# Sixty-four bytes: moving a feed-forward pool and every second staged weight tile in SBUF

## The chip, the core and the metric

The kernel runs on one core of a Trainium2 chip. It is one program: one launch takes all inputs from HBM and leaves the layer's output in HBM. The metric is the device time of one execution in microseconds. Before the change three runs gave 2179.68, 2176.11 and 2177.18 us, a median of 2177.18 us.

The engines are named as in the profile: PE (TensorE, matmuls), PEld (TensorE's loads of the stationary operand), DVE (VectorE), ACT (ScalarE), POOL (GpSimd) and SP (SyncE, which issues most DMAs here).

## The reference

One decoder layer on 512 tokens of width 2048, in float32:

```
mod = silu(c) @ w_ada + b_ada                       # six vectors of 2048
h   = rms_norm(x) * (1 + scale1) + shift1
u   = h @ w_in                                      # conv group, q, six k/v groups, gates
y   = [rms_norm(conv(u)) | rms_norm(nsa_attention(u))]
x   = x + gate1 * (y @ w_out)                       # 2048 x 2048
h   = rms_norm(x) * (1 + scale2) + shift2
x   = x + gate2 * (relu(h @ w_ff1)^2 @ w_ff2)       # 2048 x 8192, 8192 x 2048
out = rms_norm(x)
```

Most of the arithmetic is in the last two products, the feed-forward.

## The kernel before

**Precision.** Every float32 matrix is split into a high part (rounded to the type float32r) and a low part (the rest). A product of two such matrices is three matmuls into the same PSUM bank: high by high, high by low, low by high (`mm3`, L345). ACT makes the high part by a copy, DVE the low part by a subtraction.

**Operands of a matmul.** `matmul(ps, lhsT, rhs)` loads `lhsT`, 128 columns, as the stationary operand and streams `rhs`, the moving operand, past it. The profile writes a matmul as out<-moving,stationary: `pf<-tk,hl` streams tokens past feed-forward weights. In nearly all matmuls the moving operand holds tokens and the stationary one weights. In one part of the projection, the value projection (rows `ps<-wh,h` and `ps<-wl,h_m` of shape 128x268), it is the other way round: the staged weights move, 268 columns at a time, and the tokens are stationary.

**Where tiles lie.** Pools lie one behind the other in each partition of SBUF, in the order in which they are opened, and the tiles' widths give their places:

- `mainp` (L279) has 29 slots of 4096 bytes, from byte 34,816 on. Token tiles of every stage live there: `h_m`, `mix`, `mixa`, and the feed-forward's tokens `tk` (L1142).
- `attc` and `stage` follow at byte 153,600. `stage` (L283) has two pairs of tiles `wh` and `wl` (L300) and three tiles `raw` (L301), each 1088 floats, 4352 bytes. The first pair lies at 169,472 and 178,176, the second at 173,824 and 182,528. Seven token tiles `h` lie behind them.
- When the front of the layer is done, `attc` and `stage` are closed, and `ffp` (L1040), the feed-forward's pool, opens at the same byte 153,600. It holds the arriving weights `rw` (six tiles), their split parts `hl` (three tiles of a high and a low half) and `sg`, `gt`, `gb` and `p1`. All its widths are multiples of 1024 bytes.

34,816 and 153,600 are both multiples of 1024, and token slots and the offsets used within them are multiples of 512 bytes. So in the feed-forward the moving and the stationary operand of every matmul start at the same place within any 128 bytes. In the front the same holds for tokens and staged weights, but for the value projection: there a weight tile is 1072 floats, four pieces of 268 columns, so that the four pieces start 0, 1072, 2144 and 3216 bytes into the tile. Within 64 bytes these are the offsets 0, 48, 32 and 16, within 128 bytes 0, 48, 96 and 16; the token tiles, stationary there, start at 0.

**Order of the work.** An object `Order` records every operation and writes the program in an order that a planner finds by costs and due times (`price`, `plan`, `emit`). Its costs depend on shapes and on which tile names an operation touches, not on addresses. The front comes first (modulation vectors from `w_ada`, projections, attention, first half of the output projection), then from about 770 us on the feed-forward's part, which starts with the second half of the output projection.

**The feed-forward.** The two products are done by a scheme of seven products of half-size blocks. For each of 32 blocks (`ff1`, L1244) four weight tiles arrive in `rw`, DVE and ACT make seven split operands in `hl` from them (`operands`, L1197), and TensorE runs 24 matmuls of 256 columns for each (`run`, L1213). Results pass through `gt` to HBM and come back as tokens `tk` for the second product, which is built the same way. In the three blocks done first and in the last block of the second product, some operands lie in `sg` and `gt`, or in slots (`kw`).

Of the kernel before, what the change touches and what calls it, by code (L numbers as in the profile page):

```python
# [9 lines left out]
F32 = mybir.dt.float32  # L10
F32R = mybir.dt.float32r
# [5 lines left out]
P = 128  # L17
# [11 lines left out]
BLOB = 1072  # L29
SLOT = 1024  # L30
WIDE = 1088
VEC_W = 336 + 88
CST_W = 1281 - 1024 + 80
NMAIN = 29
# [238 lines left out]
def hybrid_layer(ctx: ExitStack, tc: tile.TileContext, a, out):  # L273
# [9 lines left out]
    stage = front.enter_context(tc.tile_pool(name="stage", bufs=2))  # L283

    def slot(dtype=F32, name="m"):
        return mainp.tile([P, SLOT], dtype, name=name, tag="m")
# [10 lines left out]
    vcmp = attc.tile([P, NG, 2, P], F32R, name="vcmp")  # L297
    ident_r = attc.tile([P, P], F32R, name="ident_r")
    mask_r = attc.tile([P, P], F32R, name="mask_r")
    whl = cycle([[stage.tile([P, WIDE], F32R, name=n)[:, :BLOB] for n in ("wh", "wl")] for _ in range(2)])  # L300
    wraw = cycle([stage.tile([P, WIDE], F32, name="raw", bufs=3)[:, :BLOB] for _ in range(3)])  # L301
    accs = cycle([small.tile([P, 2], F32, name="acc") for _ in range(4)])

    def temp(shape=(P, T), dtype=F32, name=None):
        t = next(temps)[:, :math.prod(shape[1:])].bitcast(dtype)
        if len(shape) == 4:
            return t.rearrange("p (a b c) -> p a b c", b=shape[2], c=shape[3])
        return t if len(shape) == 2 else t.rearrange("p (a b) -> p a b", b=shape[2])
# [23 lines left out]
    def weights(src, cols=1024, spare=False):  # L332
        raw = next(wraw)[:, :cols]
        nc.sync.dma_start(out=raw, in_=src)
        wh, wl = (slot(F32R, name="sw") for _ in range(2)) if spare else next(whl)
        wh, wl = wh[:, :cols], wl[:, :cols]
        nc.scalar.activation(wh, raw, AF.Copy)
        nc.vector.tensor_tensor(out=wl, in0=raw, in1=wh.bitcast(F32), op=OP.subtract)
        return wh, wl
# [10 lines left out]

    vec = consts.tile([P, VEC_W], F32, name="vec")[:, :V_END]
    nc.sync.dma_start(out=vec, in_=a["vec"][:, :V_END])
# [234 lines left out]
    for s, (name, k) in enumerate(steps[:-1]):  # L587
# [5 lines left out]
        wh, wl = w  # L593
# [167 lines left out]
    for j in range(8):  # L761
# [4 lines left out]
        for i in range(3):  # L766
            n = 3 * j + i
# [30 lines left out]
    for g in range(NG):  # L798
        pv = [bank() for _ in range(NQ)]
        for blk in range(4):  # L800
            wh, wl = weights(a["w_v"][g * 4 + blk], BLOB)
# [47 lines left out]
    for g in range(NG):  # L849
        pq = [bank() for _ in range(NR)]  # L850
        for k in range(NK):
            if k % 2 == 0:
                wh, wl = weights(a["w_q"][g * 8 + k // 2])
# [175 lines left out]
    while m < NK:  # L1029
# [10 lines left out]
    ffp = ffn.enter_context(tc.tile_pool(name="ffp", bufs=2, reuse_waits="tile"))  # L1040
    psf = ffn.enter_context(tc.tile_pool(name="psf", bufs=8, space=PSUM, reuse_waits="tile"))
    HT = T // 2
    rw = cycle([ffp.tile([P, 1024], F32, name="rw", bufs=6) for _ in range(6)])
    hl = cycle([ffp.tile([P, 2, 1024], F32R, name="hl", bufs=3) for _ in range(3)])
    sg = {t: cycle([ffp.tile([P, 1024], d, name="sg", bufs=2) for _ in range(2)])
          for t, d in (("first", F32R), ("sums", F32), ("last", F32R))}
    gt = cycle([ffp.tile([P, 2, 2, HT], F32R, name="gt", bufs=3) for _ in range(3)])
    gb = cycle([ffp.tile([P, 2, HT], F32R, name="gb", bufs=1)])
    p1s = cycle([ffp.tile([P, HT], F32, name="p1", bufs=3) for _ in range(3)])
    banks = cycle([psf.tile([P, T], F32, name="pf") for _ in range(8)])  # L1050
    LO, HI = slice(0, HT), slice(HT, T)
    halves = (LO, HI)
# [5 lines left out]
    def raw_blob(src):  # L1058
        raw = next(rw)
        nc.sync.dma_start(out=raw, in_=src)  # L1060
        return raw

    def hl_tile():
        t = next(hl)
        return t[:, 0], t[:, 1]

    def hilo(dst, src, minus=False):
        if minus:
            nc.scalar.activation(dst[0], src, AF.Copy, scale=-1.0)
            nc.vector.scalar_tensor_tensor(out=dst[1], in0=src, scalar=-1.0, in1=dst[0].bitcast(F32),  # L1070
                                           op0=OP.mult, op1=OP.subtract)
        else:
            nc.scalar.activation(dst[0], src, AF.Copy)
            nc.vector.tensor_tensor(out=dst[1], in0=src, in1=dst[0].bitcast(F32), op=OP.subtract)
        return dst
# [20 lines left out]
    for k in range(8):  # L1096
        wh, wl = oa[k] if k < 2 else hilo(hl_tile(), raw_blob(a["w_oa"][k]))
# [44 lines left out]
    def tslot():  # L1142
        return slot(F32R, name="tk")[:, :4 * HT].rearrange("p (k h t) -> p k h t", k=2, h=2)

# [7 lines left out]
    def normed(kp, hf):  # L1152
        c = halves[hf]
        x = x1[kp]
        t = temp((P, 2, HT), name="xr")
        nc.vector.tensor_tensor(out=t, in0=x[:, :, c], in1=r2[:, None, c].to_broadcast([P, 2, HT]),
# [252 lines left out]
    for f in range(8):  # L1409
# [7 lines left out]
        for q in range(3 if last else 4):  # L1417
            raw = [raw_blob(a["w_f2"][4 * f + q, b]) for b in range(4)]
# [127 lines left out]
```

## Time and profile before

| What | Value |
|---|---|
| median of three runs | 2177.18 us |
| the profiled execution's own time | 2177.84 us |
| its span, first to last instruction | 2176.1 us |
| TensorE clock granted over the span | 0.993 |
| PE busy | 2121.7 us, 98% |
| PEld busy | 1979.9 us, 91% |
| DVE busy | 1899.1 us, 87% |
| ACT busy | 1006.3 us, 46% |
| matmuls | 15,014 |

The span and what lies around it, 1.7 us, make the profiled execution's time, which is 0.7 us above the median. Matmuls are pipelined: each has a duration longer than its distance from the next, so distances between starts are what counts, and "PE busy" is the union of overlapping intervals. In a row of a timeline or of a chain, the time divided by the count behind the x is that distance.

### The profile page before, as it was taken

How to read it: one execution, taken by the hardware profiler on the slowest of the kernel's cores; microseconds unless marked ns; L12 is line 12 of the kernel's file. 1: busy time of each engine (PE TensorE's matmuls, PEld its weight loads, DVE VectorE, ACT ScalarE, POOL GpSimd, SP SyncE). 2: the span in 40 equal slices, each digit the busy share in tenths (PEclk: the TensorE clock that was granted, in tenths of full speed). 3: DMA queues.
4: the chain of work that ended last, by engine and by line, in shares of the span. 5: the costliest groups of instructions: out<-in, count | busy, mean ns of one | idle time of the engine just before them, and what ended most of it. 6: DMA issues, size and time to landing. Idle time of an engine off the chain costs nothing.

```text
span 2176.1 us, 37941 instructions
## 1 busy us (share of the span) xinstructions
PE 2121.7 (98%) x15014; PEld 1979.9 (91%) x15014; DVE 1899.1 (87%) x2971; ACT 1006.3 (46%) x1470; POOL 128.2 (6%) x244
## 2 busy tenths in 40 slices
PE   5999999999999999999999999999999999999997
PEld 3888778898777789999999999999999999999997
DVE  8999888888977646998898898898999999999997
ACT  4532333222544435766566566555433333333344
POOL 0000000000000000111111111111000000000000
PEclk8999999999999999999999999999999999999998
DMA  8996688877220253566656656669866366366442
GB/s 334 336 352 225 216 298 335 304 285 284 80 78 30 68 205 115 173 202 193 207 191 190 213 186 192 205 186 314 302 246 234 121 236 232 126 224 234 135 174 88
DMA packets 144129, 454.16 MB, mean 209 GB/s; under 512 B 15824, under 2 KB 20176, under 8 KB 143952
## 3 DMA queue, kind: packets, MB, share of 16 engines
q1 hardware_dynamic: 108816, 386.72, 50.8%
q0 software_dynamic: 34048, 63.98, 9.3%
q8 instruction: 118, 1.93, 0.4%
q10 hardware_dynamic: 1088, 1.05, 0.1%
q14 instruction: 59, 0.48, 0.1%
HBM read 383.53 MB, written 68.16 MB: 208 GB/s over the span
## 4 chain that ended last, share of the span: by engine, by line
PE 81%; DVE 4%; DMA 2%; ACT 1%; issue 1%; SPq 0%; DVEq 0%; ACTq 0%
PE pf L119 64%; PE ps L119 11%; PE pw L119 3%; PE pv L119 1%; DMA wa<-in_w_ada 1%; PE s L119 1%; PE pt L119 1%; DVE nm L119 1%; DMA raw<-in_cmp_w 1%; DVE t L119 0%; DVE wl L119 0%; DVE p L119 0%; DVE tt L119 0%; DVE x L119 0%; DVE sw L119 0%
## 5 line engine op out<-in xcount | busy, mean ns | idle before, releaser
L119 PE MATMUL pf<-tk,hl 128*128 128x256 f32 x10704 | 1286.8, 283 | 0.5 <-ACT t L119 0.5
L119 PEld LDWEIGHTS pf<-tk,hl 128*128 128x128 f32 x10704 | 1285.4, 192 | 0.8 <-ACT t L119 0.7
L119 ACT ACTIVATE hl<-rw 128x1024 fp32r<-128x1024 f32 x269 | 284.7, 1059 | 366.4 <-PE pf L119 264.7
L119 DVE TENSOR_TENSOR hl<-rw,hl 128x1024 fp32r<-128x1024 f32 x269 | 328.8, 1223 | 51.9 <-ACT hl L119 51.4
L119 ACT ACTIVATE hl<-sg 128x1024 fp32r<-128x1024 f32 x180 | 190.9, 1060 | 260.6 <-PE pf L119 216.2
L119 DVE SCALAR_TENSOR_TENSOR t<-wa,cs 128x1024 bf16<-128x1024 f32 x192 | 234.5, 1221 | 32.5 <-DMA wa<-in_w_ada 30.1
L119 PE MATMUL ps<-h_m,wh 128*128 128x512 f32 x720 | 223.7, 391 | 0.0
L119 ACT ACTIVATE wh<-raw 128x1024 fp32r<-128x1024 f32 (+1 forms) x106 | 112.6, 1063 | 238.5 <-PE ps L119 189.2
L119 DVE TENSOR_TENSOR hl<-sg,hl 128x1024 fp32r<-128x1024 f32 x151 | 184.8, 1224 | 40.2 <-ACT hl L119 37.5
L119 PE MATMUL ps<-h,wh 128*128 128x512 f32 x560 | 176.8, 396 | 6.4 <-ACT h L119 3.3
L119 PEld LDWEIGHTS ps<-h_m,wh 128*128 128x128 f32 x720 | 134.8, 188 | 27.5
L119 DVE SCALAR_TENSOR_TENSOR x<-pf,mod,x 128x256 f32<-128x256 f32 (+1 forms) x280 | 135.3, 488 | 23.4 <-PE pf L119 20.4
L119 DVE TENSOR_TENSOR sg<-sg,rw 128x1024 f32<-128x1024 f32 x120 | 146.1, 1218 | 0.1
L119 DVE TENSOR_TENSOR wl<-raw,wh 128x1024 fp32r<-128x1024 f32 (+1 forms) x106 | 130.0, 1226 | 13.8 <-ACT wh L119 13.1
L119 PE MATMUL ps<-h_m,wl 128*128 128x512 f32 x360 | 141.0, 392 | 0.0
L119 PEld LDWEIGHTS ps<-h,wh 128*128 128x128 f32 x560 | 106.2, 191 | 31.9 <-ACT h L119 5.3
L119 POOL DMA_DIRECT2D g<-gt x192 | 101.2, 532 | 372.5 <-issue 149.4
L119 PE MATMUL ps<-h,wl 128*128 128x512 f32 x280 | 110.5, 395 | 0.0
L119 PE MATMUL pw<-mix,wh 128*128 128x512 f32 x256 | 86.4, 403 | 0.0
L119 PEld LDWEIGHTS ps<-h_m,wl 128*128 128x128 f32 x360 | 67.8, 188 | 14.2 <-DVE wl L119 0.3
L119 ACT ACTIVATE t<-t 128x512 f32<-128x512 f32 (+3 forms) x131 | 74.5, 571 | 11.5 <-DVE t L119 9.5
L119 DVE TENSOR_TENSOR sg<-rw 128x1024 f32<-128x1024 f32 x60 | 73.2, 1219 | 5.4 <-issue 2.7
(216 smaller groups left out, 2155.2 us busy)
## 6 DMA issues: line engine op xcount, KB each, us to landing
rw<-in_w_f SPq DMA_DIRECT2D x263, 512.0 KB, 3.7
wa<-in_w_ada SPq DMA_DIRECT2D x192, 512.0 KB, 6.4
tk<-g SPq DMA_DIRECT2D x114, 512.0 KB, 6.1
g<-gt POOLq DMA_DIRECT2D x192, 256.0 KB, 3.3
raw<-in_w_conv SPq DMA_DIRECT2D x32, 512.0 KB, 4.8
x<-in_xt SPq DMA_DIRECT2D x16, 512.0 KB, 5.5
raw<-in_w_kv SPq DMA_DIRECT2D x16, 512.0 KB, 5.3
raw<-in_w_cv SPq DMA_DIRECT2D x16, 512.0 KB, 3.8
```

The costliest lines, as they stand in the source:

```text
L119: x.i, x.eng, x.call = len(self.nodes), eng, (lambda: real(*args, **kw))
```

## The change

Two things are moved in SBUF; no operation is added or taken away.

- `ffp` gets a tile of 16 floats as its first one, which nothing uses. Everything else in `ffp` then lies 64 bytes further: `rw`, `hl`, `sg`, `gt`, `gb`, `p1`. The token slots stay.
- A pair `wh`, `wl` becomes one tile of 2 x 1088 + 16 floats, 8768 bytes; the low part starts 4352 bytes behind the high part, which is a multiple of 128. The first pair's parts lie at 169,472 and 173,824, multiples of 128; the second pair's at 178,240 and 182,592, each 64 bytes past a multiple of 128. The tiles `raw` grow from 1088 to 1120 floats, so that all that follows in `stage` moves by 512 bytes in sum.

```diff
+RAW_W = 1120
+SHIFT = 16
...
-    whl = cycle([[stage.tile([P, WIDE], F32R, name=n)[:, :BLOB] for n in ("wh", "wl")] for _ in range(2)])
-    wraw = cycle([stage.tile([P, WIDE], F32, name="raw", bufs=3)[:, :BLOB] for _ in range(3)])
+    whl = [stage.tile([P, 2 * WIDE + SHIFT], F32R, name="wh") for _ in range(2)]
+    whl = cycle([[t[:, :BLOB], t[:, WIDE:WIDE + BLOB]] for t in whl])
+    wraw = cycle([stage.tile([P, RAW_W], F32, name="raw", bufs=3)[:, :BLOB] for _ in range(3)])
...
     HT = T // 2
+    ffp.tile([P, SHIFT], F32, name="shift", bufs=1)
     rw = cycle([ffp.tile([P, 1024], F32, name="rw", bufs=6) for _ in range(6)])
```

The order of the instructions on every engine and every DMA queue is the same as before, operation by operation; only the name `wl` is gone, since the low part is now half of a tile named `wh`. One wait is gone: one copy on ACT into `hl` no longer waits for an earlier instruction of ACT itself.

## The prediction

> **What bounds the kernel now.** I read the page's first two parts for the engines, the chain of waits for what sets the end, the stretches for the slack beside it, and the timeline of one stage for what an address does to a matmul.
>
> ```profile
> span 2176.1 us, 37941 instructions
> PE 2121.7 (98%) x15014; PEld 1979.9 (91%) x15014; DVE 1899.1 (87%) x2971; ACT 1006.3 (46%) x1470; POOL 128.2 (6%) x244
> PE 81%; DVE 4%; DMA 2%; ACT 1%; issue 1%; SPq 0%; DVEq 0%; ACTq 0%
> PE pf L119 64%; PE ps L119 11%; PE pw L119 3%; PE pv L119 1%; DMA wa<-in_w_ada 1%; PE s L119 1%; PE pt L119 1%; DVE nm L119 1%; DMA raw<-in_cmp_w 1%; DVE t L119 0%; DVE wl L119 0%; DVE p L119 0%; DVE tt L119 0%; DVE x L119 0%; DVE sw L119 0%
> ```
>
> TensorE sets 81% of the end, the feed-forward's matmuls (`pf`) 64% alone. From the chain in order of time, two pieces that nothing interrupts:
>
> ```profile
> 474.04 85.98 PE ps L119 x378
> 901.60 1260.63 PE pf L119 x10502
> ```
>
> The second is the feed-forward: 10,502 matmuls of 256 columns in 1260.63 us, 120.04 ns each. The first is projection work of 512 columns: 85.98 / 378 = 227.5 ns. The 256 columns between them cost 107.4 ns, 0.42 ns a column, so 256 columns alone are worth 107.4 ns and both kinds carry 12 to 13 ns on top, whatever their length. This rest, on some 11,000 feed-forward matmuls, is all that a move of addresses can touch on the path.
>
> Is that rest open to addresses? One stage of the same run answers in part. In the value projection the moving operand is a weight tile, cut into pieces of 268 columns that start 0, 48, 96 and 16 bytes into a line of 128 (0, 48, 32, 16 into 64); the stationary tokens start at 0. Each piece takes 12 matmuls, every third from the low tile. These rows of the timeline are matmuls from the low tile, by piece:
>
> ```profile
> 421.57 0.28 PE L119 MATMUL ps<-wl,h 128*128 128x268 f32 x1
> 423.01 0.29 PE L119 MATMUL ps<-wl,h 128*128 128x268 f32 x1
> ...
> 434.11 0.29 PE L119 MATMUL ps<-wl,h_m 128*128 128x268 f32 x1
> 434.87 0.29 PE L119 MATMUL ps<-wl,h_m 128*128 128x268 f32 x1
> 435.24 0.29 PE L119 MATMUL ps<-wl,h_m 128*128 128x268 f32 x1
> 436.36 0.29 PE L119 MATMUL ps<-wl,h_m 128*128 128x268 f32 x1
> 436.73 0.28 PE L119 MATMUL ps<-wl,h_m 128*128 128x268 f32 x1
> 437.83 0.28 PE L119 MATMUL ps<-wl,h_m 128*128 128x268 f32 x1
> 438.57 0.29 PE L119 MATMUL ps<-wl,h_m 128*128 128x268 f32 x1
> 439.31 0.28 PE L119 MATMUL ps<-wl,h_m 128*128 128x268 f32 x1
> ```
>
> Within a piece, from start to start:
>
> - offset 16: 434.11 to 434.87, 6 matmuls, 126.7 ns
> - offset 0: 435.24 to 436.36, 9 matmuls, 124.4 ns
> - offset 48: 436.73 to 437.83, 9 matmuls, 122.2 ns
> - offset 96: 438.57 to 439.31, 6 matmuls, 123.3 ns
>
> Same engine, same shape, same clock; only the address differs, and the distance moves by 4.5 ns. The first two rows are the lowest piece that I found: 12 matmuls in 1.44 us, 120.0 ns.
>
> **The change part by part.** No instruction is added, removed or reordered on any engine or queue, and no wait is added; nothing new stands behind a waiting instruction. One copy on ACT loses a wait for ACT's own earlier work, on an engine that is busy 46%: nothing. What is left is four effects of addresses.
>
> *Feed-forward matmuls.* Their stationary operands in the shifted pool start 64 bytes into a line of 128, the tokens at 0. These groups count:
>
> ```profile
> L119 PE MATMUL pf<-tk,hl 128*128 128x256 f32 x10704 | 1286.8, 283 | 0.5 <-ACT t L119 0.5
> L119 PE MATMUL pf<-mixa,hl x288: 277/388/498, 774.0 to 842.5; 128*128 128x512 f32 x72, 128*128 128x256 f32 x72
> ```
>
> That makes 10,992; a few smaller ones are left out. No matmul of this run has operands 64 bytes apart, so the price is bounded by the rows above. Best: the lowest piece, 120.0 ns for 268 columns, is 12 x 0.42 = 5.0 ns less for 256, that is 115.0 ns against 120.0, a gain of 5.0 ns each, 55.0 us. Worst: as the piece at 16 against that at 0, 126.7 - 124.4 = 2.3 ns more, 25.3 us. Between them nothing at all. I take the neighbours: in a line of 128 bytes, 64 lies between 48 (2.2 ns less than at 0) and 96 (1.1 ns less), and what conflict there is should be smallest farthest from 0, so I go to the upper one and round it to 2.0 ns: 10,992 x 2.0 = 22.0 us.
>
> *Front matmuls.* Every second staged pair is shifted against the tokens.
>
> ```profile
> L119 PE MATMUL ps<-h_m,wh 128*128 128x512 f32 x720 | 223.7, 391 | 0.0
> L119 PE MATMUL ps<-h,wh 128*128 128x512 f32 x560 | 176.8, 396 | 6.4 <-ACT h L119 3.3
> L119 PE MATMUL ps<-h_m,wl 128*128 128x512 f32 x360 | 141.0, 392 | 0.0
> L119 PE MATMUL ps<-h,wl 128*128 128x512 f32 x280 | 110.5, 395 | 0.0
> ```
>
> The chain has 11% + 3% of 2176.1 us, 305 us, in `ps` and `pw`: 305 / 0.2275 = 1340 matmuls of this size. Half of them shifted, 670 x 2.0 = 1.3 us. Off the chain the front waits for weights and for DVE, and a faster matmul there only waits longer.
>
> *DVE and ACT on shifted tiles.* The splits into `hl` now read and write 64 bytes further. Before, splits of the front and of the feed-forward lie at different multiples of 128 and still cost the same:
>
> ```profile
> L119 DVE TENSOR_TENSOR hl<-rw,hl 128x1024 fp32r<-128x1024 f32 x269 | 328.8, 1223 | 51.9 <-ACT hl L119 51.4
> L119 DVE TENSOR_TENSOR wl<-raw,wh 128x1024 fp32r<-128x1024 f32 x98 | 119.8, 1223 | 12.2 <-ACT wh L119 11.6
> ```
>
> I take nothing. What hides an error is DVE's slack in the feed-forward:
>
> ```profile
> 1000.00:1100.00 100.00, 100.00 (x835) 100.00 (x835) 90.13 (x121) 60.83 (x85) 18.46 (x35) 1.00 0.63 197
> 1530.00:1600.00 70.00, 70.00 (x586) 70.00 (x585) 64.48 (x87) 29.93 (x36) 5.26 (x10) 1.00 0.88 307
> 1600.00:1800.00 200.00, 200.00 (x1669) 200.00 (x1669) 184.07 (x251) 73.92 (x70) 0.00 (x0) 1.00 0.54 188
> 2000.00:2100.00 100.00, 100.00 (x836) 100.00 (x835) 94.11 (x133) 41.90 (x49) 0.00 (x0) 1.00 0.52 182
> ```
>
> DVE (the fourth number of a row) is busy 90 to 94% of these stretches. It could grow by 6% before TensorE waits for it; if that cover were gone, each further per cent on DVE costs a per cent of 1260 us, 12.6 us. The same rows say how far TensorE may gain: at 0.92 x 120 = 110 ns, late in the run at 0.94 x 120 = 113 ns, DVE becomes late next. Both lie below 115, so neither 2.0 nor 5.0 ns is cut off, though the second comes near.
>
> *DMAs into shifted tiles.* The 263 loads into `rw` now land 64 bytes further.
>
> ```profile
> rw<-in_w_f SPq DMA_DIRECT2D x263, 512.0 KB, 3.7
> wa<-in_w_ada SPq DMA_DIRECT2D x192, 512.0 KB, 6.4
> ```
>
> Over the long piece of the chain, 1260 us, 263 loads make one in about 5 us, six tiles wait in a ring, and the DMA engines (the last share in a row) are busy 52 to 88% of the stretches above. Even if a load took as long as the slowest of its size here, 6.4 us, six in flight would cover it: nothing. Without the ring it would be 2.7 us a load.
>
> *Sum.* 22.0 + 1.3 = 23.3 us off the profiled execution's own 2177.84 us (span 2176.1 and 1.7 around it): 2154.5 us. That execution lies 0.7 us above the median of 2177.18, so it stands for the runs.
>
> [...]
>
> **The rivals.**
>
> *No change, 2177 us.* An address may matter only within 64 bytes. The four pieces can be read so too: as offsets 0, 48, 32 and 16 of a line of 64, with a smooth course 124.4, 122.2, 123.3, 126.7. Then 64 more is the same place, both parts of the change do nothing, and the time is 2177 us. For it: no row separates the two readings, and the feed-forward's distance is 120.04 ns over 10,502 matmuls, stretches with ACT at 61% and at 37% alike (835 in 100 us, 1669 in 200), like something fixed. Against it: the rest above the columns isn't fixed in the value projection. [...]
>
> *The whole relief, 2119 us.* The feed-forward falls to 115.0 ns as the lowest piece: 55.0 us and 670 x 5.0 = 3.4 us, 2177.84 - 58.4 = 2119.4 us. For it: the operands' distance is the same in all 10,992 matmuls, so one good phase would hold everywhere. Against it: that piece is alone; the later ones at the same offset 0 take 124.4.
>
> *Slower, 2205 us.* The 64 bytes put weight loads and moving reads into a worse step, as offset 16 against 0: 2.3 x 10,992 = 25.3 us in the feed-forward and 670 x 2.3 = 1.5 us in the front, 2177.84 + 26.8 = 2204.6 us. Place: between matmul starts in the feed-forward. It decides from 120.5 ns on (0.4 x 10,992 = 4.4 us). For it: the equal start of today is not the worst of the four pieces, so there is room upwards. Against it: two of three other offsets are better than 0.
>
> **How the numbers follow.** Partial relief, the forecast: 0.35, with its own range 2135 to 2172 (from 40 us, most of the way to the best price, to 5 us). No change: 0.31. Whole relief: 0.16. Slower: 0.18. The three runs before span 0.16%, so 0.2%, 4.4 us, is about what a measurement of this kernel tells from no change. Faster is 0.35 + 0.16 = 0.51, the same 0.31, slower 0.18. The forecast is 2154.5 us. The range reaches from 2100 us, beyond the whole relief and short of DVE's limit, to 2185 us, over no change and the mild part of the slower case; it leaves out some 0.04 below and 0.14 above.
>
> **What would show it.** The long piece of the chain in the feed-forward: its time over its count at 118 ns or less if the forecast holds, 120.0 if 64 bytes are no distance, above 120.5 if it got worse, 115 for the whole relief. In the front the 512-column piece should fall by half the feed-forward's difference, since every second pair is shifted. DVE's share should rise from 92 to 93 or 94% in the stretches between 1600 and 2100, with busy times of single splits still at 1223 ns; loads into `rw` should land in about 3.7 us. Wrong it would be if splits or loads got longer, if TensorE began to wait for DVE, or if front and feed-forward moved in opposite directions: then address distance within a pair of operands isn't the cause.

## The result and the profile after

The changed kernel takes 2158.05 us, the median of four runs from 2157.35 to 2160.6; the kernel before takes 2176.66 us in the same comparison. The ratio is 0.9914, with a 95% interval from 0.9897 to 0.9931: 18.6 us faster, against 23.3 us forecast. (A later comparison, below, gives 0.9836 for the same kernel. Why the two differ is part of what was found.)

The page of the changed kernel, taken in the longest of its four runs (2160.6 us), with the lines that answer to those of before:

```profile
span 2158.8 us, 37940 instructions
PE 2105.8 (98%) x15014; PEld 1956.0 (91%) x15014; DVE 1889.4 (88%) x2971; ACT 1008.4 (47%) x1470; POOL 128.6 (6%) x244
PE 80%; DVE 5%; DMA 2%; ACT 1%; issue 1%; DVEq 0%; SPq 0%; ACTq 0%
L121 PE MATMUL pf<-tk,hl 128*128 128x256 f32 x10704 | 1262.3, 281 | 1.4 <-DVE hl L121 1.0
L121 DVE TENSOR_TENSOR hl<-rw,hl 128x1024 fp32r<-128x1024 f32 x269 | 327.8, 1219 | 53.6 <-ACT hl L121 53.4
rw<-in_w_f SPq DMA_DIRECT2D x263, 512.0 KB, 3.7
```

TensorE still sets the end, with 80% of the chain. Its busy time on the feed-forward's group fell from 1286.8 to 1262.3 us. The splits on DVE cost what they did (1219 against 1223 ns), and loads into `rw` land after 3.7 us as before.

The chain in order of time (start, length, what, count) shows where the time went:

```profile
452.23 111.86 PE ps L121 x570
...
907.83 633.02 PE pf L121 x5372
...
1557.59 587.93 PE pf L121 x4996
```

The long piece of before is in two. The first has 633.02 / 5372 = 117.84 ns a matmul, the second 587.93 / 4996 = 117.68, against 120.04. Over these 10,368 matmuls that is 10,368 x 120.04 - 1220.95 = 23.6 us less. But the first piece begins at 907.83 us where it began at 901.60, 6.2 us later. The difference, 17.4 us, agrees with the 17.3 us by which the span shrank. Not all of the 6.2 us can be put down to the staged pairs: in the profiles below of kernels that leave the pairs as they were, the same piece begins anywhere from 900.23 to 905.82 us. Between the two pieces lies the passage from the first product to the second, and there the slack ran out for a moment:

```profile
1530.00:1600.00 70.00, 69.03 (x593) 68.38 (x592) 65.04 (x91) 30.30 (x36) 5.28 (x10) 1.00 0.88 312
1600.00:1800.00 200.00, 200.00 (x1701) 199.90 (x1700) 187.39 (x257) 74.53 (x72) 0.00 (x0) 1.00 0.53 186
```

In these stretches (columns: length, then busy time and count of PE, PEld, DVE, ACT, POOL, then clock, DMA share, GB/s) PE idles 0.97 us between 1530 and 1600, where it had been busy all of it. DVE's share between 1600 and 1800 rose from 92% to 187.39 / 200 = 94%.

So one half of the change helped and the other seems to have hurt. The experiments take them apart, ask whether it is the distance between operands, and look at other distances. In all of them the time of the feed-forward's long piece over its count is the quantity to read.

### The profile page after: what moved, and what is told of

The parts are those of the page before. It is cut to its first block, busy times and chain, and to the rows that moved or that the text cites. A ratio compares the mean times of both kernels' runs of the same rounds, so it can differ in the third digit from the quotient of the medians.

```text
span 2158.8 us, 37940 instructions
## 1 busy us (share of the span) xinstructions
PE 2105.8 (98%) x15014; PEld 1956.0 (91%) x15014; DVE 1889.4 (88%) x2971; ACT 1008.4 (47%) x1470; POOL 128.6 (6%) x244
## 3 DMA queue, kind: packets, MB, share of 16 engines
q10 hardware_dynamic: 1088, 1.05, 0.1%
## 4 chain that ended last, share of the span: by engine, by line
PE 80%; DVE 5%; DMA 2%; ACT 1%; issue 1%; DVEq 0%; SPq 0%; ACTq 0%
PE pf L121 62%; PE ps L121 12%; PE pw L121 3%; PE pv L121 1%; PE s L121 1%; PE pt L121 1%; DVE nm L121 1%; DVE x L121 1%; DMA raw<-in_w_conv 1%; DMA raw<-in_cmp_w 1%; DVE tt L121 0%; DVE p L121 0%; DVE wh L121 0%; DVE hl L121 0%; DMA rw<-in_w_f 0%
## 5 line engine op out<-in xcount | busy, mean ns | idle before, releaser
L121 PE MATMUL pf<-tk,hl 128*128 128x256 f32 x10704 | 1262.3, 281 | 1.4 <-DVE hl L121 1.0
L121 PEld LDWEIGHTS pf<-tk,hl 128*128 128x128 f32 x10704 | 1260.1, 189 | 2.5 <-DVE hl L121 1.3
L121 DVE TENSOR_TENSOR hl<-rw,hl 128x1024 fp32r<-128x1024 f32 x269 | 327.8, 1219 | 53.6 <-ACT hl L121 53.4
L121 PE MATMUL ps<-h_m,wh 128*128 128x512 f32 x1080 | 257.0, 394 | 0.0
L121 DVE SCALAR_TENSOR_TENSOR t<-wa,cs 128x1024 bf16<-128x1024 f32 x192 | 234.2, 1220 | 19.3 <-DMA wa<-in_w_ada 17.3
L121 PEld LDWEIGHTS ps<-h_m,wh 128*128 128x128 f32 x1080 | 201.7, 188 | 45.7
L121 PE MATMUL ps<-h,wh 128*128 128x512 f32 x840 | 201.9, 396 | 5.4 <-ACT h L121 3.6
L121 PEld LDWEIGHTS ps<-h,wh 128*128 128x128 f32 x840 | 158.4, 190 | 43.5 <-ACT h L121 6.0
L121 DVE TENSOR_TENSOR wh<-raw,wh 128x1024 fp32r<-128x1024 f32 (+1 forms) x106 | 129.9, 1225 | 27.2 <-ACT wh L121 26.5
L121 PEld LDWEIGHTS pw<-mix,wh 128*128 128x128 f32 x384 | 69.5, 189 | 11.5 <-issue 0.5
L121 DVE TENSOR_TENSOR rw<-rw 128x1024 f32<-128x1024 f32 x60 | 73.0, 1217 | 0.0
L121 DVE TENSOR_TENSOR gt<-t,gt 128x512 fp32r<-128x512 f32 x96 | 65.3, 684 | 1.5 <-PE pf L121 1.5
```

The lines of the kernel that those rows point to most:

```text
L121: x.i, x.eng, x.call = len(self.nodes), eng, (lambda: real(*args, **kw))
```

## The experiments

### Each part alone

The feed-forward's part alone:

```diff
     HT = T // 2
+    ffp.tile([P, 16], F32, name="shift", bufs=1)
```

> Only the feed-forward's pool lies 64 bytes further; the staged pairs are as before. Theory A (the distance between the moving and the stationary address sets the gap between matmuls, by 64 bytes: 2.45 ns less at 256 columns, 6 ns more at 512): the feed-forward's 256-column matmuls come 117.5 ns apart as in the changed kernel, the front's 512-column ones 227 ns as before, and the time is about 2151 us, 7 us below the changed kernel. Theory B (both parts of the change help, the front's longer gaps in the changed kernel come from something else, such as later weights): 2160 us or more.

The staged pairs alone: the changed kernel without that line.

```diff
-    ffp.tile([P, SHIFT], F32, name="shift", bufs=1)
```

> Only the staged pairs are changed; the feed-forward's pool is where it was. Theory A: half of the front's 512-column matmuls come 233 ns apart in place of 227, the feed-forward's stay at 120.0, and the time is 4 to 7 us above before, about 2182 us. Theory B: 2177 us or less.

The feed-forward's part alone takes 2152.65 us, ratio 0.9884 [0.987, 0.9899]; the pairs alone 2183.11 us beside a before of 2179.79, ratio 1.0018 [1.0008, 1.0027]. Theory B, that both parts help, is out: the two work against each other. The 0.18% alone would be thin evidence, since a kernel with all distances kept shows 0.10% below; the chain carries the reading. The chain of the first:

```profile
446.84 110.37 PE ps L119 x570
...
900.23 1237.49 PE pf L119 x10502
```

and of the second:

```profile
450.93 111.86 PE ps L121 x570
...
906.90 1260.63 PE pf L121 x10502
```

The 10,502 matmuls take 1237.49 us, 117.83 ns each, with the pool shifted, and 1260.63 us, to the hundredth what they took before, without. A piece of 570 matmuls in the front, most of them of 512 columns, takes 110.37 us with the old pairs and 111.86 us with the new ones, here and in the changed kernel alike. 378 of them are the unbroken 512-column piece of before, so that is 1.49 / 378 = 3.9 ns a matmul, with one pair in two shifted. In the record of single matmuls the 512-column part runs in blocks of 24, fed by the two pairs in turn. With the old pairs every block has 226.7 ns a matmul; with the new ones the blocks have 233.3 and 227.9 in turn. So it is the shifted pair that pays most, about 6.6 ns a matmul, three times the 2.2 ns that the same 64 bytes save at 256 columns.

### Is it the distance, and of what?

The tiles in which weights arrive, but not those that TensorE reads, moved by 64 bytes. The first form of this puts the read tiles 128 bytes further as well, so that it doesn't isolate the arriving tiles after all; the second puts the read tiles 512 further.

```diff
+    ffp.tile([P, 16], F32, name="shift", bufs=1)
     rw = cycle([ffp.tile([P, 1024], F32, name="rw", bufs=6) for _ in range(6)])
+    ffp.tile([P, 16], F32, name="back", bufs=1)      # first form; 112 floats in the second
     hl = cycle([ffp.tile([P, 2, 1024], F32R, name="hl", bufs=3) for _ in range(3)])
```

> In the feed-forward only the tiles in which weights arrive lie 64 bytes further; the tiles that TensorE reads are where they were. Theory A: nothing changes, 120.0 ns and 2177 us. Theory C (the gain comes from where the loads land and where DVE and ACT read, not from the operands of a matmul): the feed-forward's distance falls towards 117.5 ns and the time towards 2151 us.

> The tiles in which feed-forward weights arrive lie 64 bytes further, and all that TensorE reads lies 512 bytes further, a distance that alternates in every kernel from one matmul to the next and made none before. In the kernel with only the arriving tiles meant to be moved, the read tiles were 128 bytes away, so it had moved both. Theory A (the operands' distance sets the gap): 120.0 ns in the feed-forward and 2178 us. Theory C (where loads land, where DVE and ACT read): near 117.7 ns and 2153 us.

Everything moved by 64 bytes, token slots, staged weights and feed-forward pool together, by a wider first tile:

```diff
-VEC_W = 336 + 88
+VEC_W = 336 + 88 + 16
```

> Everything from the small tiles on lies 64 bytes further, token slots, staged weights and the feed-forward's pool alike, so that no distance between operands changes and every address does. Theory A: 120.0 ns in the feed-forward, 227 ns in the front, 2178 us. Theory E (the address of the weights within a line sets the gap, not the distance to the tokens): 117.7 and 233 ns, about 2160 us.

The feed-forward's piece with only the arriving tiles moved (second form), and then with everything moved:

```profile
900.30 1260.68 PE pf L119 x10502
```

```profile
452.16 110.35 PE ps L119 x570
...
905.82 1260.64 PE pf L119 x10502
```

Both have 120.04 ns, and the second has the old front too. Their ratios are 1.0003 [0.9994, 1.0012] and 1.001 [1.0001, 1.0019], both within 0.2%. So neither where loads land and splits read (theory C) nor the address itself (theory E) matters. What matters is the distance between the operands of the matmuls. That DVE's and ACT's writes into the shifted tiles meet TensorE's reads of tokens would be another reading, but the single matmuls don't bear it out: with the pool shifted, between 950 and 1380 us, the 817 gaps in which neither engine writes into `hl` are 117.8 ns on average, and so are the 2834 in which one does. The first form is one of the distances below.

### Other distances

The pool 128 bytes further, and 192; the pool 32 and 96 bytes further, each with two new places for the staged pairs, whose effect the chain shows apart. A staged tile is 4480 bytes there, which isn't a multiple of 256, so the pairs lie 32 and 224 bytes past a multiple of 256 with the pool at 32, and 128 and 64 with the pool at 96 (the expectation for 96 has 192 for the second pair, but it lies at 64):

```diff
     HT = T // 2
+    ffp.tile([P, 32], F32, name="shift", bufs=1)     # 8, 24 and 48 in the others
```

```diff
-    whl = cycle([[stage.tile([P, WIDE], F32R, name=n)[:, :BLOB] for n in ("wh", "wl")] for _ in range(2)])
+    whl = cycle([[stage.tile([P, WIDE + 32], F32R, name=n)[:, o:o + BLOB] for n in ("wh", "wl")]
+                 for o in (8, 24)])                  # (32, 48) with 96
```

> The feed-forward's pool lies 128 bytes further in place of 64. Theory A with a period of 128 bytes or less: as before, 120.0 ns and 2177 us. Theory D (the gain is from any distance, or its period is 256 bytes or more): the distance differs from 120.0 ns and the time leaves 2177 us by more than 10 us.

> The feed-forward's pool lies 32 bytes further; of the staged pairs the first lies 32 and the second 96 bytes past a multiple of 128. Theory A with the value projection's pieces as a guide (offsets 48 and 96 lower than 0, 16 higher): 118 to 119 ns in the feed-forward, about 2163 us without the front. For the front's 512-column matmuls, where 64 bytes cost 6 ns, both pairs lie 32 from that: 3 ns more than 227 if the course is smooth. Theory F (only 64 has an effect, the rest as at 0): 120.0 and 227 ns, 2178 us.

> The feed-forward's pool lies 96 bytes further; the staged pairs lie 128 and 192 bytes past a multiple of 512. Theory A with a smooth course between 64 (117.7 ns) and 128 (118.7 in one execution, unstable): 118 to 118.5 ns in the feed-forward, about 2160 us without the front. In the front 128 should cost about 4 ns, as the feed-forward's few 512-column matmuls did at 128 (230.9 against 226.8), and 192 as 64, 6 ns, if the course is symmetric about 128. Theory F: 120.0 and 227 ns, 2178 us.

> Only the feed-forward's pool is moved, by 192 bytes. Theory A with a period of 256 bytes (0 and 256 are alike before, 128 is not): 192 is 64 to the other side. If the sign of the distance does not matter, 117.7 ns and 2153 us; if the course falls from 128 on back to 0, between 118.7 and 120.0 ns and 2165 to 2178 us.

The chain at 32 bytes:

```profile
453.00 112.79 PE ps L119 x570
...
910.33 606.08 PE pf L119 x5119
...
1562.56 591.89 PE pf L119 x4996
```

at 96:

```profile
452.23 112.63 PE ps L119 x570
...
908.36 1246.70 PE pf L119 x10502
```

at 128, and in the first form above, whose read tiles lie 128 bytes away too:

```profile
901.21 1247.15 PE pf L119 x10502
```

```profile
905.08 1254.27 PE pf L119 x10502
```

and at 192:

```profile
901.71 1237.87 PE pf L119 x10502
```

| Pool's distance, bytes | ns per 256-column matmul | Time, us (runs, from to) | Ratio |
|---|---|---|---|
| 0 (before) | 120.04 | 2177 to 2180 by comparison | 1 |
| 32 (both pairs shifted too) | 118.4 | 2168.49 (4, 2167.11 to 2169.86) | 0.9954 [0.9938, 0.9971] |
| 64 | 117.83 | 2152.65 (4, 2152.36 to 2155.84) | 0.9884 [0.987, 0.9899] |
| 96 (both pairs shifted too) | 118.71 | 2170.68 (5, 2167.72 to 2172.0) | 0.9963 [0.995, 0.9976] |
| 128 | 118.75 | 2169.23 (10, 2163.47 to 2179.93) | 0.9959 [0.994, 0.9977] |
| 128 (first form above) | 119.43 | 2176.23 (10, 2166.27 to 2186.06) | 0.9985 [0.9965, 1.0005] |
| 192 | 117.87 | 2155.98 (4, 2154.68 to 2156.64) | 0.9899 [0.9884, 0.9914] |

Theory F, only 64 does anything, is out: every distance tried between 0 and 256 shortens the feed-forward's gap, at least over part of an execution. The course isn't smooth: 32 and 96 lie above 64. And 128 is no return to 0, so nothing repeats every 128 bytes; theory D's 10 us at 128 came just about (10.6 us below the before of its own comparison). 256 is like 0 in the kernel before, whose second staged pair lies 256 bytes off the first in 512 and has the same 226.7 ns in the front. At 256 columns the two sides of 0 then agree: 64 and 192 have the same gap.

In the front, shifting both pairs costs 112.79 - 110.35 = 2.44 us in the 570 (6.5 ns on the 378), for 32 and 224 bytes, where 3 ns were expected; 128 and 64 cost 2.28 us (6.0 ns). The feed-forward has a few 512-column matmuls too (144 in `pf<-mixa,hl`). In the records of single matmuls they come 226.8 ns apart at 0, 233.3 at 32, 233.4 at 64, 234.3 at 96, 232.4 at 128 and 229.0 at 192, the last in one profile alone. At 512 columns every distance tried between 0 and 256 is worse than 0, and the two sides of 0 do not agree.

At 128 the runs spread over 16 and 20 us where those of the kernels so far spread over 2 to 7. Stretches of the first form's profile show why:

```profile
1000.00:1200.00 200.00, 200.00 (x1669) 200.00 (x1668) 180.17 (x239) 120.29 (x170) 36.51 (x70) 1.00 0.63 197
1600.00:1800.00 200.00, 200.00 (x1688) 200.00 (x1687) 183.93 (x252) 74.80 (x71) 0.00 (x0) 1.00 0.54 195
```

A stretch also counts a matmul or two that reach over its edges. Read singly, the gaps of the first stretch are 120.0 ns on average, those of the second 118.7. The 120.0 is the average of distance 0, but not its pattern: the single gaps repeat 117, 120, 123, where at 0 nearly all are 119 to 121. Those of the second run through 115 to 122 in a repeated order. The same matmuls at the same distance run at either of two speeds, for hundreds of microseconds at a time.

### Two rhythms

The last comparison put a new distance for the low parts beside the changed kernel and its better half, all on one chip. The new one keeps the pool 64 bytes further and puts the low part of each split another 128 bytes away, 192 in all:

```diff
     HT = T // 2
+    ffp.tile([P, 16], F32, name="shift", bufs=1)
...
-    hl = cycle([ffp.tile([P, 2, 1024], F32R, name="hl", bufs=3) for _ in range(3)])
+    hl = cycle([ffp.tile([P, 2, 1024 + 32], F32R, name="hl", bufs=3)[:, :, :1024] for _ in range(3)])
```

> The feed-forward's pool lies 64 bytes further, and within each split pair the low part another 128 bytes, so that the weights read one after the other lie 64, 64 and 192 bytes from the tokens. Theory A, each gap set by its own matmul's distance: near 117.7 ns if 192 is like 64, and a mean between if it is not. Theory G (the gap is set by a rhythm that many equal matmuls fall into): another value, unsteady from run to run.

> The changed kernel once more, on the chip and beside the runs of the next one. 2158 us.

> The feed-forward's part of the change alone once more. If the staged pairs' part costs what the chain of the changed kernel says, this is 4 to 7 us below the changed kernel in the same call, 2153 us; if the earlier difference was the chip's, it is 2158 us.

The first takes 2116.52 us (four runs from 2113.12 to 2117.87), ratio 0.9716 [0.9701, 0.973], faster than the kernel before and the changed one:

```profile
939.99 538.72 PE pf L119 x4751
...
1533.16 500.47 PE pf L119 x4408
```

That is 113.4 and 113.5 ns. No mean of the 117.83 and 117.87 that 64 and 192 gave alone makes it, so theory A as it was put, each gap set by its own matmul's distance, fails against those values. Theory G expected another value, which came, and unsteady runs, which didn't: these four lie within 4.8 us. But whether the low parts' 192 bytes make the new value is not shown, since 64 alone reaches it too in the same comparison, as the next two kernels show. That the mixed distances hold it more surely rests on four runs and one profile.

The changed kernel takes 2137.92 us this time (four runs from 2134.28 to 2158.85, ratio 0.9836 [0.9788, 0.9885]), its feed-forward half 2132.69 us (2118.99 to 2140.02, 0.9804 [0.9783, 0.9824]). Both expectations, 2158 and 2153, were missed by 20 us. The changed kernel's chain:

```profile
904.95 592.47 PE pf L121 x5028
...
1553.84 503.30 PE pf L121 x4432
```

The first piece has the 117.83 ns of its first profile; the second 113.56. The feed-forward's half goes to and fro within one execution:

```profile
1200.00:1350.00 150.00, 150.00 (x1326) 150.00 (x1326) 141.05 (x191) 96.11 (x133) 29.09 (x55) 1.00 0.68 209
1420.00:1500.00 80.00, 80.00 (x681) 80.00 (x680) 70.10 (x97) 47.11 (x67) 12.07 (x23) 1.00 0.84 291
1600.00:1800.00 200.00, 200.00 (x1767) 200.00 (x1766) 190.81 (x263) 77.64 (x73) 0.00 (x0) 1.00 0.61 215
```

1326 in 150 us are 113.1 ns, 681 in 80 us are 117.5, 1767 in 200 us are 113.2 (singly 113.3, 117.8 and 113.3). The granted clock is 1.00 in all three, and in all stretches shown above. So at 64 bytes there are two steady gaps, 117.8 and 113.3 ns. In the first comparisons the changed kernel and its half, with four runs each (2157 to 2161 and 2152 to 2156 us), had kept mostly to the longer. Mostly, because the shorter stands in the changed kernel's first profile too, hidden in the mean of its second piece:

```profile
1566.40:1599.00 32.60, 32.60 (x288) 32.51 (x287) 30.48 (x42) 13.13 (x14) 2.64 (x5) 1.00 0.97 345
```

That is 113.2 ns. Read singly, this rhythm begins near 1561 us and ends at 1604.49, where two gaps of 206 and 194 ns stand; from there on it is 117.8. In the kernel's later profile it begins at about the same place, no such gaps stand near 1604, and it lasts to 2100 us.

In the feed-forward half's execution, too, the record of single matmuls shows the gap changing at pauses: at 1396 us, for instance, two gaps of 139 and 194 ns stand between 113, 113, 114 before and 117, 118, 118 after, and nothing drifts between pauses. The kernel with the low parts at 192 came back to 113.3 after the pauses of its profiled execution. What decides which rhythm is caught after a pause was not found. The longest run of the changed kernel in this comparison, 2158.85 us, suggests that the faster rhythm is not sure on this chip either; whether chips differ in how often it is caught can't be told from these runs.

What the front's half of the change costs was to come out of this comparison too. The medians differ by 5.2 us, as expected, but with both kernels spread over more than 20 us that proves nothing; the chains and the blocks of single matmuls carry it.

## Why the prediction was right, and where it was not

The time, 2158.05 us, lies 3.5 us above the forecast and within the likeliest case's range. The terms:

- **Feed-forward matmuls.** Forecast 2.0 ns less on 10,992, 22.0 us. Measured 120.04 - 117.76 = 2.3 ns (1220.95 us over 10,368), 25.1 us on as many. The term was right and somewhat small, for the slower of the two rhythms at 64 bytes. That the first four runs kept mostly to that rhythm is luck: the same kernel later took 2137.92 us, 39 us below its before, with some 4400 matmuls at 113.56 ns, and the forecast knew of no such state. That the matmul is touched through its operands' distance, which the sum presumed, is shown: moving everything, or the arriving tiles alone, leaves 120.04 ns.
- **The choice of 2.0 ns between neighbours.** The step "what conflict there is should be smallest farthest from 0" in a line of 128 bytes gave a good number for a poor reason; that too is luck. The runs at 32, 96, 128 and 192 show no such course and no period of 128: 128 is not 0. And a distance doesn't have one price: 64 has two (117.8 and 113.3 ns), and 128 has two (120.0 and 118.7). The four pieces were no price list either, since the same offset 0 stands there with 120.0 and with 124.4 ns.
- **Front matmuls.** This step failed. It carried the 2.0 ns from 256 to 512 columns, on the argument that both kinds have the same 12 to 13 ns on top, and expected 1.3 us of gain. At 512 columns the 64 bytes cost: 6.6 ns a matmul from the shifted pair, and 0.18% (about 4 us) for the pairs alone. The long feed-forward piece began 6.2 us later in the changed kernel and 5.3 us later with the pairs alone, but kernels with the old pairs differ there by as much. An equal rest at distance 0 didn't mean an equal response. In the total the error of this term is some 5 us by the runs and 7.5 at most by the profiles, and the feed-forward term, 3 us too small, hid part of it.
- **DVE, ACT and DMA.** Forecast nothing, and splits (1219 ns) and loads (3.7 us) are as they were. DVE's share of the stretch from 1600 to 1800 rose to 94%, the upper end of what was forecast. One microsecond of PE waiting for DVE at the passage between the two products is new. It is one of the signs that were to show the prediction wrong; the prediction had DVE late only near 110 to 113 ns, by its share over whole stretches.
- **The rival of no change** is out by the change itself and by every kernel with the pool's read tiles at a distance between 0 and 256 but the first 128-byte form, whose interval includes 1. The trace's four pieces of the value projection could be read by lines of 64 or 128 bytes; neither reading was right.
- **The rival of the whole relief** had the right size and was not refuted: 115.0 ns and 2119 us were estimated from the lowest piece, and the second rhythm has 113.3 ns. The feed-forward's half ran once in 2118.99 us. It is a state that can be caught, not a price.
- **The slower rival** expected longer gaps between matmuls, at the wrong place: they were to be in the feed-forward and came in the front.
- **The sign that was to refute** it, front and feed-forward moving in opposite directions, came, and the conclusion set on it, that distance isn't the cause, was wrong: with everything moved together both parts return to their old gaps (110.35 us for the 570 in the front, 120.04 ns in the feed-forward).

The same instructions at another distance between the two operands run 113.3, 117.8 or 120.0 ns apart; 113.3 ns is the shortest steady gap that these trains showed. The runs show that the distance matters, not by what means it does.

## What to carry to other kernels

Where long trains of equal matmuls, each with its own weight load, run with all tiles laid out at multiples of large powers of two, the distance in bytes between moving and stationary operand is worth a sweep: it costs nothing to change, and 64 and 192 bytes in the feed-forward alone, or both together, were worth 1.0% to 2.8% here (32, 96 and 128 bytes at most 0.5%). Sweep it for each matmul length apart, since the 64 bytes that saved 2 to 7 ns a matmul at 256 columns cost 6.6 ns at 512, and don't move two parts in one step without reading them apart in the chain. And read the gap over several executions and stretches before you believe a small difference, since the same program held one of two steady gaps, which shifted its time by 20 us and more.

## What was not expected of the hardware

- The average gap has steady values, not a spread: 120.04 ns at distance 0 over 10,502 matmuls; 117.8 or 113.3 at 64; 120.0 or 118.7 at 128; 117.87 at 192; 113.4 with 64 and 192 mixed. The single gaps of a rhythm are nearly equal (0, 64) or repeat a pattern (128). A rhythm lasts for tens to hundreds of microseconds, and where single gaps were read it changed at a pause of TensorE, some as short as 0.1 to 0.2 us.
- At 113.3 ns DVE is busy 190.81 of 200 us, 95%, and TensorE still doesn't wait for it in that stretch (200.00 of 200.00 busy).
